# Pooling mixer on plain 32-bit operands, and the last feed-forward's first weights split on VectorE between the norms

## The chip, the cores and the metric

One core of a Trainium2 chip runs the whole program. The metric is the device time of one execution in microseconds (us); a kernel's time is the median of its runs.

## What is computed

One inference step of a backbone of two layers: feed-forward, token mixer, feed-forward, with an RMS norm and a modulation before and an RMS norm and a gate after each. The first layer's mixer is a recurrent scan, the second layer's a pooling mixer. The change is in the pooling mixer and in the feed-forward behind it (the fourth and last). Cut to that:

```python
def rms_norm(x, g):
    return x * lax.rsqrt(jnp.mean(x * x, axis=-1, keepdims=True) + RMS_EPS) * g

def premod(x, g_pre, shift, scale):
    return rms_norm(x, g_pre) * (1 + scale) + shift

def pool_mix(h, pool_w, pool_scale, grid):      # windows 2, 4, 8, 16 for four groups of 256 channels
    for gi, win in enumerate(POOL_WINDOWS):
        part = h[..., gi * POOL_GC:(gi + 1) * POOL_GC]
        m = part
        for ax in axes:
            m = centred_box_mean(m, win, ax)
        outs.append(m - part)
    y = jnp.einsum('...gc,gce->...ge', jnp.stack(outs, axis=-2), pool_w)
    return y.reshape(B, T, D) * pool_scale

        out = pool_mix(h, W['pool_w'][j], W['pool_scale'][j], grid)
        x = x + m[5] * rms_norm(out, W['norm_post'][i, 1])
        h = premod(x, W['norm_pre'][i, 2], m[6], m[7])
        f = (silu(h @ w1) * (h @ w3)) @ w2
        x = x + 0.5 * m[8] * rms_norm(f, W['norm_post'][i, 2])
```

There are 640 tokens (512 on a grid of width 64, and 128 in a row), 1024 channels, and a feed-forward width of 2816.

## The kernel before

Activations lie channels by tokens: `x` is 8 tiles of 128 channels by 640 tokens. The tokens are handled in two halves, half 0 of 384 and half 1 of 256 (`HALF`), nearly everywhere one after the other. Most matmuls are made three times, on operands split into a high and a low part of the type fp32r: high by high, high by low, low by high (`mm3`, lines L299 to L301). So each weight tile of 128x1024 is loaded by a transfer (L290, queue of SyncE), cast to its high part on ScalarE (L293) and has that subtracted on VectorE or GpSimd (L294) (`wsplit`). The table `EARLY` says which of a feed-forward's first weight tiles have the subtraction on GpSimd.

A feed-forward has 22 pieces of 128 rows. Its first part (`ffn_s1`) multiplies the activations by the pieces of w1 and w3, its second (`ffn_s2`) the product by those of w2, half 0 and then half 1. Behind the second part a postnorm (L232 to L243) scales the result and adds it to `x`.

A prenorm squares `x` on ScalarE (L211), adds the squares on VectorE (L215), sums them over channels on TensorE (L178), makes the reciprocal root on VectorE (L181 to L192), spreads it over partitions on TensorE (L194), multiplies `x` by it on VectorE (L257) and applies scale and shift on ScalarE (L266) with a few pieces on GpSimd (L264). `prenorm` then casts each of the 8 tiles to its high part on ScalarE (L275) and subtracts it on VectorE (L276).

The pooling mixer (`PoolMix`) works in another order than the formula, since mixing channels and averaging over tokens commute:

- `load_weights` loads the two tiles of mixing weights, casts them on ScalarE (L1161) and subtracts on VectorE (L1162).
- `mix` multiplies, for each of the five blocks of 128 tokens, the normed activations by them: 8 products of 256 columns for each block, three times each (L1201 to L1203). The result z is cast (L1205) and subtracted (L1206) into a high and a low tile. These ten tiles live in the six pairs of buffers of the feed-forward's split weights ("wh", "wl").
- `window` multiplies z by matrices of zeros and ones that stand for the box sums (L1223). These are loaded (L1169) and converted to fp32r on GpSimd, the last seven on ScalarE (L1171).
- its `postnorm` multiplies by the reciprocal counts (L1234, VectorE), squares (L1237, ScalarE), adds up the squares (L1241, VectorE), and, with the reciprocal root, scales (L1245, VectorE) and adds to `x` (L1247, in turn on GpSimd and VectorE).

The tile framework keeps the engines' queues: a list scheduler sets the order of each engine's instructions when the program is built, each engine then executes its own list strictly in that order, and an instruction waits for the tiles that it reads and for the buffer that it writes. So an instruction that waits holds up all behind it on its engine, and on SyncE's queue a transfer that waits for its buffer holds up those behind it. The raw weight tiles have four buffers.

## Time and profile before

| what | value |
|---|---|
| time, median of 3 runs | 3035.88 us (3034.88 to 3042.86) |
| the profiled execution's own time | 3045.13 us |
| its span, first to last instruction | 3043.2 us |
| TensorE matmul busy | 2860.9 us (94%) |
| VectorE busy | 1836.1 us (60%) |
| ScalarE busy | 1078.8 us (35%) |
| GpSimd busy | 478.8 us (16%) |
| DMA, mean over the span | 126 GB/s |

The profile is one execution. Its engines are PE (TensorE; PEld is its weight load), DVE (VectorE), ACT (ScalarE), POOL (GpSimd) and SP (SyncE). L followed by a number is a line of the kernel before. PEclk is the clock that TensorE was granted, as a share of 2.4 GHz: 1.00 is the upper of its two levels, 0.50 the lower, 1.2 GHz. All times of a timeline count from the start of the span. The pooling stage and the start of the last feed-forward lie between about 2440 and 2600 us.

### The profile page before, as it was taken

To read this page: it belongs to the slowest core of one execution; us is meant where nothing else is said; L and a number is where in the kernel's file an instruction comes from. 1 tells how busy PE (TensorE), PEld (TensorE's weight loads), DVE (VectorE), ACT (ScalarE), POOL (GpSimd) and SP (SyncE) were. 2 spreads that over 40 slices of the span, in tenths; PEclk is the share of its full clock that TensorE was granted. 3 is DMA by queue.
4 is the path that set the end of the run, shared out by engine and by line. 5 is a ranking of instruction groups with operands and counts; after the bars stand their busy time and mean duration, and the time that the engine had idled before them with its cause. 6 is when DMAs were issued, how large, how long until landed. Compare 5 with 4: busy or idle time off the path is not lost.

```text
span 3043.2 us, 52485 instructions
## 1 busy us (share of the span) xinstructions
PE 2860.9 (94%) x21086; PEld 2567.0 (84%) x21086; DVE 1836.1 (60%) x3662; ACT 1078.8 (35%) x1892; POOL 478.8 (16%) x530
## 2 busy tenths in 40 slices
PE   8999999898899999998799999999999986999997
PEld 5999998585566666667689999999999986999997
DVE  7997328835666776664879992763232678423336
ACT  3112234234444454544431123542122454312233
POOL 2000033121001011101400003310002433000034
PEclk9999999998788898887899999999999987999999
DMA  6665234435333443114336663332223432222233
GB/s 245 198 219 179 84 126 142 157 118 167 115 90 107 118 119 113 42 31 139 114 122 212 228 221 132 125 113 81 72 77 111 139 107 80 90 77 70 92 123 125
DMA packets 163733, 382.02 MB, mean 126 GB/s; under 512 B 22433, under 2 KB 84513, under 8 KB 163233
## 3 DMA queue, kind: packets, MB, share of 16 engines
q1 hardware_dynamic: 161472, 375.60, 37.9%
q8 instruction: 165, 2.70, 0.4%
q10 hardware_dynamic: 2016, 3.07, 0.3%
q14 instruction: 80, 0.65, 0.1%
HBM read 352.19 MB, written 26.41 MB: 124 GB/s over the span
## 4 chain that ended last, share of the span: by engine, by line
PE 75%; DVE 12%; ACT 5%; issue 4%; DMA 4%; POOL 1%; SPq 0%; DVEq 0%; ACTq 0%; POOLq 0%
PE ps L300 17%; PE ps L299 17%; PE ps L301 17%; PE px L667 4%; PE pg L811 2%; DVE cj L113 2%; PE pa L739 1%; DVE t L215 1%; PE pc L949 1%; PE px L638 1%; ACT gg L897 1%; DMA mid<-xs 1%; PE ps L502 1%; ACT t L266 1%; DVE wl L294 1%
## 5 line engine op out<-in xcount | busy, mean ns | idle before, releaser
L299 PE MATMUL ps<-hp,wh 128*128 128x384 f32 (+2 forms) x3008 | 934.1, 312 | 17.3 <-ACT hp L275 10.4
L300 PE MATMUL ps<-hp,wh 128*128 128x384 f32 (+2 forms) x3008 | 935.4, 312 | 5.7 <-DVE hp L483 2.1
L301 PE MATMUL ps<-hp,wl 128*128 128x384 f32 (+2 forms) x3008 | 930.9, 310 | 3.3 <-DVE wl L294 3.1
L294 DVE TENSOR_TENSOR wl<-raw,wh 128x1024 fp32r<-128x1024 f32 x353 | 438.7, 1247 | 468.5 <-ACT wh L293 468.0
L293 ACT ACTIVATE wh<-raw 128x1024 fp32r<-128x1024 f32 x369 | 389.4, 1059 | 831.7 <-PE ps L300 693.0
L299 PEld LDWEIGHTS ps<-hp,wh 128*128 128x128 f32 x3008 | 571.0, 190 | 20.9 <-ACT hp L275 12.6
L300 PEld LDWEIGHTS ps<-hp,wh 128*128 128x128 f32 x3008 | 572.7, 190 | 8.2 <-DVE hp L483 2.3
L301 PEld LDWEIGHTS ps<-hp,wl 128*128 128x128 f32 x3008 | 570.0, 190 | 5.6 <-DVE wl L294 5.3
L350 POOL TENSOR_TENSOR gl<-t,gh 128x384 fp32r<-128x384 f32 (+1 forms) x176 | 236.3, 1344 | 1564.4 <-ACT gh L349 1534.3
L301 PE MATMUL ps<-gh,wl 128*128 128x384 f32 (+1 forms) x1408 | 438.3, 312 | 4.1 <-DVE wl L294 4.1
L300 PE MATMUL ps<-gl,wh 128*128 128x384 f32 (+1 forms) x1408 | 436.3, 310 | 3.1 <-POOL gl L350 3.1
L299 PE MATMUL ps<-gh,wh 128*128 128x384 f32 (+1 forms) x1408 | 436.0, 310 | 2.6 <-ACT gh L349 2.6
L113 DVE CUSTOM_DVE_ANT_0 cj<-raw,cj,bmod 128x1024 bf16<-128x1024 f32 x264 | 341.4, 1293 | 13.5 <-DMA raw<-in_w_mod 9.5
L301 PEld LDWEIGHTS ps<-gh,wl 128*128 128x128 f32 x1408 | 269.0, 191 | 5.2 <-DVE wl L294 4.3
L300 PEld LDWEIGHTS ps<-gl,wh 128*128 128x128 f32 x1408 | 268.5, 191 | 5.0 <-POOL gl L350 4.3
L299 PEld LDWEIGHTS ps<-gh,wh 128*128 128x128 f32 x1408 | 268.8, 191 | 4.4 <-ACT gh L349 3.2
L323 ACT ACTIVATE t<-ps 128x384 f32<-128x384 f32 (+1 forms) x176 | 75.5, 429 | 382.2 <-PE ps L301 382.2
L667 PE MATMUL px<-mid,pw 128*128 128x320 f32 x448 | 184.3, 525 | 9.8 <-DMA mid<-xs 7.0
L325 DVE TENSOR_TENSOR t<-t,ps 128x384 f32<-128x384 f32 (+1 forms) x176 | 85.4, 485 | 156.3 <-PE ps L301 155.8
L324 DVE SCALAR_TENSOR_TENSOR t<-t,ps 128x384 f32<-128x384 f32 (+1 forms) x176 | 85.1, 483 | 119.3 <-ACT t L323 119.3
L667 PEld LDWEIGHTS px<-mid,pw 128*128 128x128 f32 x448 | 84.2, 217 | 46.4 <-issue 16.2
L349 ACT ACTIVATE gh<-t 128x384 fp32r<-128x384 f32 (+1 forms) x176 | 79.9, 457 | 53.6 <-PE ps L301 30.2
(372 smaller groups left out, 3444.6 us busy)
## 6 DMA issues: line engine op xcount, KB each, us to landing
raw<-in_w SPq DMA_DIRECT2D x352, 512.0 KB, 3.3
raw<-in_w_mod SPq DMA_DIRECT2D x132, 512.0 KB, 4.2
mid<-xs SPq DMA_DIRECT2D x224, 160.0 KB, 2.3
pw<-in_w_rkv SPq DMA_DIRECT2D x28, 256.0 KB, 3.3
raw<-in_w_o SPq DMA_DIRECT2D x9, 512.0 KB, 5.7
d<-po SPq DMA_DIRECT2D x28, 160.0 KB, 2.3
w<-in_w_mod_first SPq DMA_DIRECT2D x8, 512.0 KB, 7.7
raw<-in_w_rkv SPq DMA_DIRECT2D x8, 512.0 KB, 4.9
```

The costliest lines, as they stand in the source:

```text
L113: nc.vector.tensor_tensor_reduce(self.junk, w, self.cond[:, i], 0.5, self.bmod[:, layer, idx, k:k + 1], ALU.mult, ALU.add, out[:, k, i:i + 1])
L293: nc.scalar.activation(h, w, AF.Copy)
L294: (eng or nc.vector).tensor_tensor(l, w, h, op=ALU.subtract)
L299: nc.tensor.matmul(out, wh, xh, start=start, stop=False)
L300: nc.tensor.matmul(out, wh, xl, start=False, stop=False)
L301: nc.tensor.matmul(out, wl, xh, start=False, stop=stop)
L323: nc.scalar.activation(gt, o[0], AF.Tanh, scale=0.5)
L324: nc.vector.scalar_tensor_tensor(gt, gt, 1.0, o[0], op0=ALU.add, op1=ALU.mult)
L325: nc.vector.tensor_tensor(gt, gt, o[1], op=ALU.mult)
L349: nc.scalar.activation(gh, g, AF.Copy)
L350: nc.gpsimd.tensor_tensor(gl, g, gh, op=ALU.subtract)
L667: nc.tensor.matmul(p[:, 0:320], w[k // 4][:, k % 4 * P:k % 4 * P + P], x, start=k == 0, stop=k == KD - 1)
```

## The change

The mixing weights are loaded as they are and used in 32 bits, and so are the normed activations of the pooling mixer (`prenorm_plain`), so that each product is made once. The casts and subtractions of both go. The mixed tiles z of the fifth block move to the buffer "cj", which is free by then, so that two of the six pairs of weight buffers are free during the mixing. Of the last feed-forward the first three pieces (six weight tiles) are split on VectorE, `EARLY[2]` being empty, and asked for with `fetch` by hand: piece 0 behind half 0's prenorm, piece 1 before half 1's postnorm, piece 2 behind it. Line numbers shift by a few (L294 becomes L300, L1171 L1176, L1234 L1238, L1241 L1245, L1245 L1249, L1247 L1251), and the mixing matmuls are L1207.

```diff
--- before.py
+++ after.py
@@ -35,7 +35,7 @@
 PB = (5, 6, 7, 3, 1, 2, 0, 4)
 SQ = (0, 2, 4, 6)
 XD = (1, 3, 5, 7)
-EARLY = ((), (0, 1, 2, 3, 4, 5), (0, 1, 2, 3, 4, 5))
+EARLY = ((), (0, 1, 2, 3, 4, 5), ())
 
 
 class Net:
@@ -278,6 +278,12 @@
             lo.append(l)
         return hi, lo
 
+    def prenorm_plain(self, hf, gs, sh, bank=None):
+
+        h = [self.part(hf, k, 0, F32) for k in range(KD)]
+        self.prenorm_to(hf, gs, sh, lambda k, _: [(a, b, cd, h[k][:, a:b]) for a, b, cd in SEGS[hf]], bank)
+        return h
+
     def prenorm_to(self, hf, gs, sh, dest, bank=None):
         for _ in self.prenorm_gen(hf, gs, sh, dest, bank):
             pass
@@ -306,9 +312,12 @@
         g = [[None] * NFF, [None] * NFF]
         ws = {}
 
-        def step(f, hf):
+        def fetch(f):
             if f not in ws:
                 ws[f] = [self.wsplit(t["w13"][fi, f, i], nc.gpsimd if 2 * f + i in early else None) for i in range(2)]
+
+        def step(f, hf):
+            fetch(f)
             hi, lo = hs[hf]
             n = HALF[hf][1] - HALF[hf][0]
             o = []
@@ -330,7 +339,7 @@
         order = [(f, h) for h in (lead, 1 - lead) for f in range(3)]
         for f in range(3, NFF):
             order += [(f, 0), (f, 1)]
-        return order, step, g
+        return order, step, g, fetch
 
     def ffn_s2(self, wsrc, gsrc, nk, hf):
         nc, t = self.nc, self.t
@@ -1154,13 +1163,9 @@
         n, nc = self.n, self.nc
         self.ws = []
         for j in range(2):
-            w = n.wp.tile([P, 1024], F32, tag="wh", name=n.name("pw"), bufs=n.nw)
+            w = n.raw([P, 1024])
             nc.sync.dma_start(w, self.t["pool_w"][j])
-            h = n.wp.tile([P, 1024], F32R, tag="raw", name=n.name("pwh"), bufs=n.nraw)
-            l = n.wp.tile([P, 1024], F32R, tag="raw", name=n.name("pwl"), bufs=n.nraw)
-            nc.scalar.activation(h, w, AF.Copy)
-            nc.vector.tensor_tensor(l, w, h, op=ALU.subtract)
-            self.ws.append((h, l))
+            self.ws.append(w)
 
     def load_box(self, hf, lo=0, hi=None):
         n, nc, t = self.n, self.nc, self.t
@@ -1185,22 +1190,21 @@
     def mix(self, hf, h):
 
         n, nc = self.n, self.nc
-        hi, lo = h
         for j in range((HALF[hf][1] - HALF[hf][0]) // P):
-            zh = n.wp.tile([P, 1024], F32R, tag="wh", name=n.name("zh"), bufs=n.nw)
-            zl = n.wp.tile([P, 1024], F32R, tag="wl", name=n.name("zl"), bufs=n.nw)
+            if 3 * hf + j < 4:
+                zh, zl = (n.wp.tile([P, 1024], F32R, tag=s, name=n.name("z"), bufs=n.nw) for s in ("wh", "wl"))
+            else:
+                z = n.main.tile([P, 4 * NT], F32R, tag="cj", name=n.name("z"))
+                zh, zl = z[:, 0:1024], z[:, 1024:2048]
             ts = slice(j * P, (j + 1) * P)
             for q in range(2):
                 p = n.psum()
-                wh, wl = self.ws[q]
                 for g in range(2):
                     for kk in range(2):
                         s = slice((g * 2 + kk) * 256, (g * 2 + kk) * 256 + 256)
                         k = (2 * q + g) * 2 + kk
                         o = p[:, g * 256:g * 256 + 256]
-                        nc.tensor.matmul(o, hi[k][:, ts], wh[:, s], start=kk == 0, stop=False)
-                        nc.tensor.matmul(o, hi[k][:, ts], wl[:, s], start=False, stop=False)
-                        nc.tensor.matmul(o, lo[k][:, ts], wh[:, s], start=False, stop=kk == 1)
+                        nc.tensor.matmul(o, h[k][:, ts], self.ws[q][:, s], start=kk == 0, stop=kk == 1)
                 es = slice(q * 512, q * 512 + 512)
                 nc.scalar.activation(zh[:, es], p, AF.Copy)
                 nc.vector.tensor_tensor(zl[:, es], p, zh[:, es], op=ALU.subtract)
@@ -1266,7 +1270,7 @@
         n.fp, n.ntmp = c.enter_context(tc.tile_pool(name=n.name("fp"), bufs=1)), NFF
 
     def run_ffn(i, hs, todo, l, s, after, wait=0, early=(), begun=None):
-        order, step, g = begun or n.ffn_s1(i, hs, 0, early)
+        order, step, g, _ = begun or n.ffn_s1(i, hs, 0, early)
         todo = list(todo)
         for q, (f, hf) in enumerate(order):
             if g[hf][f] is None:
@@ -1402,7 +1406,7 @@
                 hold["gs"] = gs_sh(1, 1)
             if hf == 1:
                 pm.load_weights()
-            h = n.prenorm(hf, *hold["gs"], bank)
+            h = n.prenorm_plain(hf, *hold["gs"], bank)
             if hf == 0:
                 pm.load_box(0)
                 pm.load_rc(0)
@@ -1417,12 +1421,19 @@
         pm.load_rc(1)
         for hf in range(2):
             pm.mix(hf, hp[hf])
-        hs = []
+        hs = [None, None]
+        begun = n.ffn_s1(3, hs, 0, EARLY[2])
         for hf in range(2):
             o, bank = pm.window(hf)
+            if hf:
+                begun[3](1)
             pm.postnorm(o, hf, gp, bank)
-            hs.append(n.prenorm(hf, gs, sh, bank))
-        run_ffn(3, hs, [], 1, 2, lambda hf, bank: n.store_x(y_out, hf), early=EARLY[2])
+            if hf:
+                begun[3](2)
+            hs[hf] = n.prenorm(hf, gs, sh, bank)
+            if hf == 0:
+                begun[3](0)
+        run_ffn(3, hs, [], 1, 2, lambda hf, bank: n.store_x(y_out, hf), begun=begun)
 
 
 def pack_pool(i):
```

The order of the instructions that results, at two places. First VectorE while half 0's squares are added up behind the pooling mixer (`t_24240`, in the changed kernel `t_24103`, is the sum). Before:

```order
L215 TENSOR_TENSOR t_24240<-t_24240,t_24242 128x384
L1247 TENSOR_TENSOR x_13843<-x_13843,t_24195 128x384
L215 TENSOR_TENSOR t_24240<-t_24240,t_24245 128x384
L1234 TENSOR_TENSOR t_24407<-ps_24343,t_23925 128x256
L215 TENSOR_TENSOR t_24240<-t_24240,t_24248 128x384
L215 TENSOR_TENSOR t_24240<-t_24240,t_24251 128x384
L1234 TENSOR_TENSOR t_24411<-ps_24343,t_23925 128x256
L215 TENSOR_TENSOR t_24240<-t_24240,t_24254 128x384
L215 TENSOR_TENSOR t_24240<-t_24240,t_24257 128x384
L1234 TENSOR_TENSOR t_24416<-ps_24344,t_23927 128x256
L215 TENSOR_TENSOR t_24240<-t_24240,t_24260 128x384
L1241 TENSOR_TENSOR t_24409<-t_24409,t_24413 128x256
```

Now:

```order
L215 TENSOR_TENSOR t_24103<-t_24103,t_24105 128x384
L1251 TENSOR_TENSOR x_13843<-x_13843,t_24058 128x384
L215 TENSOR_TENSOR t_24103<-t_24103,t_24108 128x384
L300 TENSOR_TENSOR wl_24285<-raw_24282,wh_24284 128x1024
L215 TENSOR_TENSOR t_24103<-t_24103,t_24111 128x384
L300 TENSOR_TENSOR wl_24291<-raw_24288,wh_24290 128x1024
L215 TENSOR_TENSOR t_24103<-t_24103,t_24114 128x384
L1238 TENSOR_TENSOR t_24294<-ps_24218,t_23869 128x256
L215 TENSOR_TENSOR t_24103<-t_24103,t_24117 128x384
L1238 TENSOR_TENSOR t_24298<-ps_24218,t_23869 128x256
L215 TENSOR_TENSOR t_24103<-t_24103,t_24120 128x384
L1238 TENSOR_TENSOR t_24303<-ps_24219,t_23871 128x256
```

The two subtractions of piece 1 (`wl_24285`, `wl_24291`) now stand among the additions of the sum; before, the subtractions of these weights were in GpSimd's list.

Second SyncE's queue of transfers while half 1 is mixed and half 0's window runs (`in_w` with the name `raw` is the feed-forward's weights, `in_box_b` the window matrices of half 1). Before:

```order
L1169 DMA t_23897<-in_box_b 128x256
L290 DMA raw_24601<-in_w 128x1024
L290 DMA raw_24607<-in_w 128x1024
L1169 DMA t_23901<-in_box_b 128x256
L290 DMA raw_24667<-in_w 128x1024
L290 DMA raw_24673<-in_w 128x1024
L1169 DMA t_23905<-in_box_b 128x256
L290 DMA raw_24733<-in_w 128x1024
L1169 DMA t_23909<-in_box_b 128x256
L1169 DMA t_23913<-in_box_b 128x256
L1169 DMA t_23917<-in_box_b 128x256
L1169 DMA t_23921<-in_box_b 128x256
```

Now:

```order
L1174 DMA t_23841<-in_box_b 128x256
L1174 DMA t_23845<-in_box_b 128x256
L296 DMA raw_24282<-in_w 128x1024
L296 DMA raw_24288<-in_w 128x1024
L1174 DMA t_23849<-in_box_b 128x256
L296 DMA raw_24379<-in_w 128x1024
L296 DMA raw_24385<-in_w 128x1024
L1174 DMA t_23853<-in_box_b 128x256
L1174 DMA t_23857<-in_box_b 128x256
L1174 DMA t_23861<-in_box_b 128x256
L1174 DMA t_23865<-in_box_b 128x256
```

The two weight tiles of piece 0 no longer stand here; they are asked for earlier, among the first window matrices of half 0. Four weight tiles (pieces 1 and 2) stand where four stood before (pieces 0 and 1), ahead of the last four window matrices.

## Rows read from the trace of the kernel before

**Rows 1.** The page, part 4: the chain that ended last, share by engine.

```profile
PE 75%; DVE 12%; ACT 5%; issue 4%; DMA 4%; POOL 1%; SPq 0%; DVEq 0%; ACTq 0%; POOLq 0%
```

**Rows 2.** Stretches: us, then busy (instructions) of PE, PEld, DVE, ACT, POOL; PEclk, DMA, GB/s.

```profile
2476.80:2487.35 10.55, 9.72 (x81) 9.28 (x80) 9.28 (x32) 4.18 (x9) 0.12 (x1) 1.00 0.05 17
...
2502.90:2510.50 7.60, 7.59 (x48) 7.60 (x49) 4.93 (x14) 7.22 (x20) 1.39 (x2) 0.73 0.21 68
...
2525.95:2545.47 19.52, 3.13 (x15) 2.64 (x13) 19.31 (x23) 10.29 (x17) 15.41 (x9) 0.54 0.33 107
```

**Rows 3.** Timeline of PE at the last feed-forward's start: start, length, line, [idle before <- releaser].

```profile
2545.47 1.44 PE L178 MATMUL ps<-inv_d,t 128*128 128x2 f32 x6 [13.48 <-DVE t L215]
...
2593.15 0.38 PE L300 MATMUL ps<-hp,wh 128*128 128x256 f32 x1 [0.25 <-DVE hp L276]
```

**Rows 4.** Timeline of DVE, half 0's sum of squares behind the pooling mixer.

```profile
2531.56 2.45 DVE L215 TENSOR_TENSOR t<-t,t 128x384 f32<-128x384 f32 x1
...
2535.20 2.70 DVE L215 TENSOR_TENSOR t<-t,t 128x384 f32<-128x384 f32 x1
...
2538.16 4.99 DVE L215 TENSOR_TENSOR t<-t,t 128x384 f32<-128x384 f32 x2
...
2544.86 0.55 DVE L215 TENSOR_TENSOR t<-t,t 128x384 f32<-128x384 f32 x1
2545.33 2.57 DVE L1241 TENSOR_TENSOR t<-t,t 128x256 f32<-128x256 f32 x1
```

**Rows 5.** Timeline of POOL in the same stretch.

```profile
2534.83 7.91 POOL L294 TENSOR_TENSOR wl<-raw,wh 128x1024 fp32r<-128x1024 f32 x3
```

**Rows 6.** Line L294 in the pooling stage, ns min/median/max.

```profile
L294 DVE TENSOR_TENSOR wl<-raw,wh x11: 1216/1226/1824, 2434.9 to 2597.6; 128x1024 fp32r<-128x1024 f32 x11
...
L294 POOL TENSOR_TENSOR wl<-raw,wh x6: 2356/2611/2666, 2512.7 to 2545.0; 128x1024 fp32r<-128x1024 f32 x6
```

**Rows 7.** Timeline of ACT in the pooling stage.

```profile
2446.21 0.92 ACT L275 ACTIVATE hp<-t 128x384 fp32r<-128x384 f32 x2
...
2504.14 1.25 ACT L266 ACTIVATE t<-t,mall,gall 128x128 f32<-128x128 f32 x3
2505.30 0.71 ACT L275 ACTIVATE hp<-t 128x256 fp32r<-128x256 f32 x2
...
2511.55 1.06 ACT L293 ACTIVATE wh<-raw 128x1024 fp32r<-128x1024 f32 x1
```

**Rows 8.** Timeline of PE, third feed-forward's tail.

```profile
2453.57 0.62 PE L299 MATMUL ps<-gh,wh 128*128 128x256 f32 x3 [1.32 <-ACT gh L349]
2454.51 0.39 PE L300 MATMUL ps<-gl,wh 128*128 128x256 f32 x1 [0.32 <-POOL gl L350]
```

**Rows 9.** Timeline of DVE ahead of the third feed-forward's last postnorm.

```profile
2471.08 1.23 DVE L1162 TENSOR_TENSOR pwl<-pw,pwh 128x1024 fp32r<-128x1024 f32 x1 [2.66 <-ACT pwh L1161]
```

**Rows 10.** Timeline of PE in the channel mixing of half 0.

```profile
2482.03 0.28 PE L1201 MATMUL ps<-pwh,hp 128*128 128x256 f32 x1
...
2485.43 0.28 PE L1201 MATMUL ps<-pwh,hp 128*128 128x256 f32 x1
```

**Rows 11.** Timeline of PE: plain 32-bit matmuls at the lower and the upper clock.

```profile
581.71 2.28 PE L502 MATMUL ps<-t,w 128*128 128x382 f32 x3 [8.02 <-DVE t L466]
...
593.79 1.26 PE L502 MATMUL ps<-t,w 128*128 128x260 f32 x5
```

**Rows 12.** Line L502 by stretch: us, busy of PE, of PEld, granted clock, DMA, GB/s.

```profile
582.00:583.00 1.00, 1.00 (x2) 0.55 (x2) 0.50 0.00 0
594.00:595.00 1.00, 1.00 (x5) 0.58 (x4) 1.00 0.50 146
```

**Rows 13.** Line L502, ns min/median/max.

```profile
L502 PE MATMUL ps<-t,w x144: 382/383/1004, 550.7 to 607.6; 128*128 128x260 f32 x80, 128*128 128x382 f32 x64
```

**Rows 14.** The chain of waits in order of time, around half 0's window.

```profile
2511.43 7.48 DMA t<-in_box_b
...
2521.16 0.84 PE ps L178 x6
```

## Prediction

> **What bounds the kernel now.** I read the page's chain of waits first: TensorE holds 75% of it, VectorE 12% [rows 1], so a change outside TensorE pays only where TensorE waits. The change touches one place, about 2440 to 2600 us, so I cut that into stretches [rows 2]. The reader is to see two kinds. While half 0 is mixed (2476.8 to 2487.4) TensorE is busy 9.72 of 10.55 us, but so is VectorE with 9.28. Behind the pooling mixer (2525.95 to 2545.47) TensorE works 3.13 of 19.52 us and VectorE 19.31: there VectorE is the bound. Then the timelines say what the waits end on: TensorE stands still for 13.48 us until the sum of squares L215 is there [rows 3], and this is the longest wait of the place.
>
> **Why VectorE is slow there.** An L215 of 384 columns takes 0.55 us at 2544.86, but 2.45, 2.70 and twice 2.5 us between 2531 and 2543 [rows 4]. In just this time GpSimd subtracts weights, three in 7.91 us [rows 5], and each stretched addition ends about when one of those does. GpSimd's subtraction takes 2.61 us, VectorE's 1.23 [rows 6].
>
> **The change part by part.** My sum is made against the profiled execution's 3045.13 us, which is 9.25 us above the median of 3035.88; I take the same saving off either.
>
> *a. The tail of the third feed-forward.* ScalarE's 8 casts L275 of half 0's activations, 0.46 us each [rows 7], 3.7 us in all, are gone. Behind them in ScalarE's list stood the cast gh for which TensorE waited 1.32 us, and GpSimd's gl after it, 0.32 us [rows 8]. With 3.7 us less ahead of gh both waits vanish: 1.6 us. Bounds: 0 if the next weight is late instead, 1.6 otherwise, since no other wait stands there. VectorE's 8 subtractions go too; they cost nothing here, as TensorE covers them.
>
> *b. The postnorm before the mixing.* VectorE can take the first bank of results only when it is through with L1162, which waits 2.66 us for the cast of the mixing weights and ends at 2472.3 [rows 9]. TensorE finishes one bank of 18 matmuls each 18 x 0.113 = 2.04 us (the spacing of such products: 30 steps from 2482.03 to 2485.43 [rows 10]), the last at 2476.8, so the first was there at 2476.8 - 3 x 2.04 = 2470.7. Without L1162 VectorE starts 1.6 us sooner, and TensorE's list, which has the norm's small matmuls among the mixing, waits on VectorE. I take those 1.6; bounds 0 (another wait takes its place) and 2.
>
> *The mixing matmuls themselves.* Half 0 had 72 products at 0.113 us, 8.1 us; now 24. For a plain 32-bit product the nearest rows are those of the recurrent mixer's projections: five of 260 columns in 1.26 us, three of 382 in 2.28 [rows 11], the former at granted clock 1.00 and the latter at 0.50 [rows 12]. The last of a group runs to its own end, 0.38 us at the shortest and 1.00 at the longest [rows 13], so the spacings are (1.26 - 0.38)/4 = 0.22 us and (2.28 - 1.00)/2 = 0.64, and for 256 columns 0.22 and 0.43. So 24 x 0.22 = 5.3 us, 2.8 us less TensorE work. I count this at nothing, as VectorE's 9.28 us cover it: TensorE only waits longer for the norm in its midst.
>
> *c. Half 1: prenorm, mixing, half 0's window.* TensorE takes each tile as ScalarE casts it, and in the 7.60 us of this mixing ScalarE is busy 7.22 [rows 2]. Eight casts of 0.35 go, 2.8 us; the 12 pieces L266 that stay are 12 x 0.42 = 5.0 us [rows 7]. TensorE now has 16 products for 48: at the lower level 16 x 0.43 = 6.9 us, at the upper 3.5; the stretch had 0.73. Behind it ScalarE has two casts of piece 0 instead of one, 1.06 us more [rows 7], and VectorE two subtractions, 2.4 us, where it had stood waiting for ScalarE. What ended this stretch was a window matrix that landed 7.48 us after it was asked for [rows 14], behind four weight tiles in the queue; the queue has four ahead of it again, the first of them released by the end of the mixing, so it comes earlier as the mixing does. I take 2.8 - 1.1 = 1.7. Bounds: 0 (the matrices land no earlier) and 2.8.
>
> *d. Half 0's sum of squares.* Without GpSimd's subtractions four additions shrink to 0.55 us: (2.45 - 0.55) + (2.70 - 0.55) + (4.99 - 1.10) = 7.9 us. Two subtractions of piece 1 enter VectorE's list among them, 2 x 1.23 = 2.5 us; nothing else there changes its count. 7.9 - 2.5 = 5.4, and I take 5.5 with a little for VectorE's update of `x`. Bounds 3 (ScalarE, which now casts three weight tiles ahead of the last square instead of two, becomes the slower) and 8 (the two fit into gaps).
>
> *e. From that sum to the last feed-forward.* The stretched L1241 ends at 2545.33 + 2.57 = 2547.90 [rows 4], 1.0 us behind TensorE's sums L178, which end at 2545.47 + 1.44 = 2546.91 [rows 3], and the norm's first step waits for it. This 1.0 goes, one subtraction of 1.23 us comes in, and the sixth lies under TensorE's spreading of the norm: -0.2. Bounds -1.2 and 1.0.
>
> *The rest.* Half 1's norm is made while TensorE works on half 0's first pieces; it waited 0.25 us for it [rows 3]. That cover moves along with the start and stays. The end of the kernel is the same.
>
> Sum: 1.6 + 1.6 + 1.7 + 5.5 - 0.2 = **10.2 us**. Profiled 3034.9, median **3025.7**. The bounds add up to 1.8 and 15.4.
>
> **The rivals.** *The transfers hold it.* If the last window matrices come no earlier, or ScalarE's casts of piece 0 and 1 hold the squares, c gives 0 and d 3: 1.6 + 1.6 + 3 - 0.2 = 6.0, 3029.9. For it speaks that the DMA link is the chain's longest single one there, 7.48 us [rows 14], and that ScalarE gets three casts ahead of the last square; against it, that two of the six tiles now land before the mixing.
>
> *Four passes.* Spacing at 0.43 us at the upper level and 0.87 at the lower, if a plain 32-bit product took twice what I read. Mixing half 0 would be 24 x 0.43 = 10.3 us, 2 us more than before, and half 1 about 4 us longer than I reckon: 10.2 - 2 - 4 = 4.2, 3031.7. Against it: 0.22 us for 260 columns at 2.4 GHz are two cycles for a column [rows 11], though this is another place of the kernel. The Trainium skill states this rule (FP8 and Floating Point Precision, section TensorE Precision Notes): true FP32 goes through the array in four passes. The rows here speak against it; by it the time would be that of this rival.
>
> *A ring of waits makes it slower.* ScalarE's cast of piece 1 (wh) stands ahead of five of the eight squares, and its buffer is one that holds z until TensorE's last window matmuls are through; these wait for window matrices that ScalarE converts itself, and whose transfers stand in the queue behind weight tiles that wait for VectorE's subtractions of piece 0. Each us by which the last matrix comes later than I reckon makes the sum of squares a us later: from 10.2 us on the change loses, and at 20 us the time is 3025.7 + 20 = 3045.7. Against it: the worst landing that the chain shows here was 7.48 us [rows 14], with four weight tiles ahead as now.
>
> *More than reckoned.* If the matrices land at once and the two subtractions fit into gaps: 1.6 + 2 + 2.8 + 8 + 1.0 = 15.4, 3020.5.
>
> **How the numbers follow.** About 0.3% (9.1 us) is what a measurement of this kernel can tell from no change, so the bounds of "same" are 3026.8 and 3045.0. My forecast (9.1 to 13 us saved) has 0.45, more than that 0.13: faster 0.58. Transfers or ScalarE 0.27, four passes 0.05, other losses of a and b 0.05: same 0.37. The ring, 0.05: slower. The three runs of before lie 8 us apart, so the range is 3018.5 to 3033.0: it takes in the larger gain and the transfers, and reaches into the four passes, and leaves out some 2 in 10.
>
> **What would show it.** In the changed profile: no wait on gh in the third feed-forward's tail; L1207 spaced 0.22 us at clock 1.00; every L215 of half 0 near 0.55 us, and no GpSimd subtraction of weights between 2500 and 2560; TensorE's wait of 13.48 us down to 7 to 9; about 5 us gained by the first norm behind the window, 10 by the last feed-forward's first matmul. I am wrong if L215 stays above 2 us without GpSimd beside it, if L1207 is spaced 0.43 at clock 1.00, or if the gain of the place is given back within the last feed-forward.

## Result and the profile after

| | before | after |
|---|---|---|
| median of the runs shown together, us | 3034.99 (3028.22 to 3047.93, 12 runs) | 3019.62 (3010.37 to 3034.76, 12 runs) |
| ratio to before, 95% interval | | 0.995 [0.9936, 0.9965] |
| the same kernel timed a second time (run again, below) | 3030.86 (35 runs) | 3021.72 (12 runs), 0.9971 [0.9958, 0.9984] |
| profiled execution, us (its span) | 3045.13 (3043.2) | 3018.19 (3016.4) |
| TensorE busy, us | 2860.9 | 2849.8 |
| VectorE busy, us | 1836.1 | 1821.1 |
| GpSimd busy, us | 478.8 | 462.2 |

The change is faster in both comparisons, by the medians 15.4 us in the first (10.6 to 19.4 by its interval) and 9.1 us in the second (4.9 to 12.7). I had forecast 10.2 us and 3025.7, with a range of 3018.5 to 3033.0.

The page's chain of waits [rows 1]: TensorE's share is up from 75% to 78%, VectorE's down from 12% to 11%.

```profile
PE 78%; DVE 11%; ACT 4%; issue 3%; DMA 3%; POOL 1%; SPq 0%; ACTq 0%; DVEq 0%; POOLq 0%
```

The two profiled executions lie 26.8 us apart in span, but not all of it is the change: 17.8 us stand already at the sums L178 of the norm ahead of the third feed-forward's tail (2435.03 and 2417.22), and up to there both programs issue the same instructions. So I measure from there. Call **the place** the way from these sums to the last feed-forward's first product, and cut it at rows that both traces have: the first mixing product of half 0, that of half 1, the sum of squares behind half 0's window (L178 in six steps), half 0's next sum (L178), the first product.

| stretch, us | before | after | forecast and measured |
|---|---|---|---|
| a: tail of the third feed-forward | 41.88 | 39.50 | 1.6, got 2.4 |
| b and the norm of c: mixing half 0 to mixing half 1 | 26.00 | 24.35 | |
| rest of c: to the sum behind half 0's window | 18.25 | 18.46 | b + c 3.3, got 1.4 |
| d: to half 0's sum of squares | 24.31 | 17.83 | 5.5, got 6.5 |
| e: to the last feed-forward's first product | 11.50 | 11.65 | -0.2, got -0.15 |
| the place | 121.94 | 111.79 | 10.2, got 10.15 |
| from there to the end | 486.23 | 487.39 | 0, got -1.2 |

Three stretches of after in the view of stretches (us; busy and instructions of PE, PEld, DVE, ACT, POOL; granted clock, DMA share, GB/s), for the three of [rows 2]:

```profile
2456.88:2465.91 9.03, 9.01 (x43) 7.53 (x43) 7.47 (x28) 3.54 (x7) 0.00 (x0) 1.00 0.00 1
...
2481.07:2489.78 8.71, 8.71 (x33) 7.44 (x34) 3.75 (x10) 7.15 (x17) 1.34 (x3) 0.82 0.08 31
...
2504.32:2517.36 13.04, 2.19 (x14) 1.70 (x12) 13.04 (x25) 9.12 (x16) 4.76 (x4) 0.65 0.23 75
```

While half 0 is mixed TensorE now works 9.01 of 9.03 us, and in half 1's mixing 8.71 of 8.71. Whether it also sets the pace there, the run one_pass asks below. Behind half 0's window TensorE still stands while VectorE is busy from end to end, but for 13.04 us in place of 19.52.

TensorE's timeline at the waits of [rows 3, 8], with what ended each in brackets:

```profile
2449.45 0.38 PE L306 MATMUL ps<-gl,wh 128*128 128x256 f32 x1 [0.64 <-POOL gl L359]
...
2517.36 1.44 PE L178 MATMUL ps<-inv_d,t 128*128 128x2 f32 x6 [8.43 <-DVE t L215]
2524.90 1.65 PE L194 MATMUL ps<-dg,ones 128*128 128x384 f32 x2 [6.10 <-DVE dg L192]
...
2529.01 1.33 PE L305 MATMUL ps<-hp,wh 128*128 128x384 f32 x3 [1.82 <-ACT hp L275]
```

The wait of 1.32 us on gh and that of 0.32 us on gl behind it are gone. The 0.64 us on gl are those of the tail's last piece, which the kernel before has too (0.43 us at 2469.44; the prediction left it out). The 13.48 us for the sum of squares are 8.43. The same timeline in the mixing, for [rows 10], and under it all of line L1207 (ns, shortest, median, longest):

```profile
2456.72 4.05 PE L1207 MATMUL ps<-raw,hp 128*128 128x256 f32 x18
...
2481.07 8.71 PE L1207 MATMUL ps<-raw,hp 128*128 128x256 f32 x32 [1.07 <-POOL hp L264]
```

```profile
L1207 PE MATMUL ps<-raw,hp x80: 377/379/796, 2456.7 to 2489.4; 128*128 128x256 f32 x80
```

The source has 40 products at L1207, the trace 80 matmul records: a plain 32-bit product leaves two. 18 records in 4.05 us, the last of 0.38, are (4.05 - 0.38) / 17 = 0.216 us for a record and 0.43 for a product, at a granted clock of 1.00. My 0.22 us for a product was the time of a record.

VectorE's timeline through half 0's sum of squares and the first steps of the norm behind it, for [rows 4]:

```profile
2509.92 0.84 DVE L215 TENSOR_TENSOR t<-t,t 128x384 f32<-128x384 f32 x1
...
2511.15 0.55 DVE L215 TENSOR_TENSOR t<-t,t 128x384 f32<-128x384 f32 x1
2511.62 1.21 DVE L300 TENSOR_TENSOR wl<-raw,wh 128x1024 fp32r<-128x1024 f32 x1
2512.75 0.55 DVE L215 TENSOR_TENSOR t<-t,t 128x384 f32<-128x384 f32 x1
2513.22 1.22 DVE L300 TENSOR_TENSOR wl<-raw,wh 128x1024 fp32r<-128x1024 f32 x1
...
2515.16 0.55 DVE L215 TENSOR_TENSOR t<-t,t 128x384 f32<-128x384 f32 x1
...
2519.66 0.16 DVE L183 TENSOR_SCALAR ms<-ms 128x3 f32<-128x3 f32 x1
2519.73 0.15 DVE L186 TENSOR_TENSOR a<-yi 128x3 f32<-128x3 f32 x1
2519.80 0.42 DVE L1238 TENSOR_TENSOR t<-ps,t 128x256 f32<-128x256 f32 x1
2520.14 0.15 DVE L187 TENSOR_TENSOR a<-a,ms 128x3 f32<-128x3 f32 x1
2520.20 1.22 DVE L300 TENSOR_TENSOR wl<-raw,wh 128x1024 fp32r<-128x1024 f32 x1
```

No L215 takes more than 0.84 us. The one of 0.84 us ends at 2510.76, 0.41 us after an addition of GpSimd:

```profile
2509.10 1.25 POOL L1251 TENSOR_TENSOR x<-x,t 128x384 f32<-128x384 f32 x1 [0.26 <-DVE t L1249]
```

Among VectorE's additions stand the two subtractions that I had counted, and the norm's small steps (L183 to L187) take turns with half 1's L1238 and another subtraction. The chain of waits around half 0's window (start, length), for [rows 14]:

```profile
2481.07 8.71 PE ps L1207 x32
2489.78 9.73 PE ps L1227 x65
2499.53 0.84 PE ps L178 x6
```

TensorE's own products follow each other here; the window matrix, whose landing was a link of 7.48 us before, isn't in the chain any more.

### The profile page after: what moved, and what is told of

It reads as the page before. It is cut to its first block, busy times and chain, and to the rows that moved or that the text cites. A ratio compares the mean times of both kernels' runs of the same rounds, so it can differ in the third digit from the quotient of the medians.

```text
span 3016.4 us, 52355 instructions
## 1 busy us (share of the span) xinstructions
PE 2849.8 (94%) x21046; PEld 2557.6 (85%) x21046; DVE 1821.1 (60%) x3650; ACT 1070.1 (35%) x1874; POOL 462.2 (15%) x524
## 4 chain that ended last, share of the span: by engine, by line
PE 78%; DVE 11%; ACT 4%; issue 3%; DMA 3%; POOL 1%; SPq 0%; ACTq 0%; DVEq 0%; POOLq 0%
PE ps L306 18%; PE ps L305 18%; PE ps L307 18%; PE px L676 4%; PE pg L820 2%; DVE cj L113 2%; PE pa L748 1%; PE pc L958 1%; PE px L647 1%; DVE t L215 1%; ACT gg L906 1%; DMA mid<-xs 1%; PE ps L511 1%; DVE wl L300 1%; PE pc L966 1%
## 5 line engine op out<-in xcount | busy, mean ns | idle before, releaser
L305 PE MATMUL ps<-hp,wh 128*128 128x384 f32 (+2 forms) x3008 | 932.2, 312 | 15.0 <-ACT hp L275 10.4
L300 DVE TENSOR_TENSOR wl<-raw,wh 128x1024 fp32r<-128x1024 f32 x359 | 446.8, 1248 | 472.6 <-ACT wh L299 471.9
L305 PEld LDWEIGHTS ps<-hp,wh 128*128 128x128 f32 x3008 | 569.5, 190 | 18.4 <-ACT hp L275 12.2
L113 DVE CUSTOM_DVE_ANT_0 cj<-raw,cj,bmod 128x1024 bf16<-128x1024 f32 x264 | 341.4, 1293 | 12.8 <-DMA raw<-in_w_mod 8.8
```

The costliest lines, as they stand in the source:

```text
L113: nc.vector.tensor_tensor_reduce(self.junk, w, self.cond[:, i], 0.5, self.bmod[:, layer, idx, k:k + 1], ALU.mult, ALU.add, out[:, k, i:i + 1])
L300: (eng or nc.vector).tensor_tensor(l, w, h, op=ALU.subtract)
L305: nc.tensor.matmul(out, wh, xh, start=start, stop=False)
```

## Experiments

All places and ends below come from one profile each. The sum of both is the best figure, as it leaves out what lies ahead. The two executions of the changed kernel (after and again) differ by 0.1 us in the place and by 1.6 us in the sum, so sums that lie 2 us apart tell little.

| run | a | b, norm | rest of c | d | e | place | to the end | sum |
|---|---|---|---|---|---|---|---|---|
| before | 41.88 | 26.00 | 18.25 | 24.31 | 11.50 | 121.94 | 486.23 | 608.2 |
| after | 39.50 | 24.35 | 18.46 | 17.83 | 11.65 | 111.79 | 487.39 | 599.2 |
| again | 39.73 | 24.34 | 18.38 | 17.79 | 11.66 | 111.90 | 485.70 | 597.6 |
| gpsimd_splits | 38.70 | 25.33 | 19.66 | 24.17 | 10.77 | 118.63 | 486.75 | 605.4 |
| vector_splits | 41.75 | 25.02 | 18.00 | 17.02 | 13.25 | 115.04 | 486.75 | 601.8 |
| plain_only | 39.61 | 25.43 | 19.38 | 24.19 | 10.77 | 119.38 | 486.49 | 605.9 |
| no_early_fetch | 39.65 | 24.27 | 19.82 | 17.03 | 12.76 | 113.53 | 484.65 | 598.2 |
| one_pass | 39.73 | 24.45 | 17.68 | 18.30 | 11.66 | 111.82 | 487.94 | 599.8 |
| norm_first | 39.90 | 23.81 | 19.92 | 15.54 | 8.99 | 108.16 | 498.17 | 606.3 |

**again: the changed kernel once more.** No edit.

> The changed kernel, unchanged. Call the place the stretch of TensorE's work from its first product behind the last sum of squares of half 0's norm ahead of the third feed-forward's tail to the last feed-forward's first product: 120.3 us in the profile of before, 109.9 in that of after. The two profiles lie 26.9 us apart, though, and 17.6 of this stand already ahead of the place, where the two programs are the same. Theory A: what lies ahead differs from execution to execution, and the change is worth what the place and the last feed-forward show, 9 to 10.5 us; the median then comes to 0.9965 to 0.997 of before, and in the traces of these four kernels the start of the place scatters by 10 us or more without regard to the edit. Theory B: the whole difference of the medians, 15.4 us, belongs to the change (something ahead of the place runs faster); then the ratio comes to 0.995 again, and the place starts about 5 us or more sooner in every kernel with plain operands. Within the place both expect 109.9 +- 1.

Measured: 3021.72 us, ratio 0.9971 [0.9958, 0.9984]. The place is 111.9 us (1.9 less in the count of the expectation, which begins at the first product behind the sums). In the nine profiles of the table it starts at 2435.0, 2417.2, 2421.3, 2429.4, 2419.7, 2416.3, 2423.4, 2413.9 and 2411.1 us, in the table's order, though no edit touches what lies ahead. Theory B wanted an earlier start with plain operands, but gpsimd_splits, with them, starts at 2429.4 and vector_splits, without them, at 2419.7. So theory A holds: 9.0 and 10.6 us by the sums are the change, and the profiles differ by up to 24 us ahead of it, those of the changed kernel alone by 4.1.

**gpsimd_splits: the subtractions back on GpSimd.**

```diff
-EARLY = ((), (0, 1, 2, 3, 4, 5), ())
+EARLY = ((), (0, 1, 2, 3, 4, 5), (0, 1, 2, 3, 4, 5))
```

> The changed kernel with the weights of the last feed-forward's first three pieces subtracted on GpSimd again. Theory 1 (an addition of VectorE is stretched while GpSimd subtracts): three or more of half 0's L215 take 2.4 us or more again, the place takes 115 to 118 us (6.5 us of the 10.4 are lost), the time rises by 5 to 8 us against the changed kernel. Theory 2 (the additions waited for something else, such as ScalarE's squares, and the earlier fetch cured it): L215 stays at 0.55 to 0.85 us, the place at 110 +- 1.

VectorE's timeline of this run in half 0's sum of squares, then GpSimd's:

```profile
2523.50 2.33 DVE L215 TENSOR_TENSOR t<-t,t 128x384 f32<-128x384 f32 x1
...
2527.03 2.71 DVE L215 TENSOR_TENSOR t<-t,t 128x384 f32<-128x384 f32 x1
...
2529.99 4.98 DVE L215 TENSOR_TENSOR t<-t,t 128x384 f32<-128x384 f32 x2
```

```profile
2523.07 2.35 POOL L300 TENSOR_TENSOR wl<-raw,wh 128x1024 fp32r<-128x1024 f32 x1 [0.66 <-ACT wh L299]
...
2526.65 7.91 POOL L300 TENSOR_TENSOR wl<-raw,wh 128x1024 fp32r<-128x1024 f32 x3
```

Four L215 are at 2.3 to 2.7 us again, each through about 0.4 us after one of GpSimd's subtractions (the second: 2527.03 + 2.71 = 2529.74, against 2526.65 + 7.91 / 3 = 2529.29). Stretch d is 24.17 us, as before. Theory 1 holds for the additions and the place. The time is another matter: the median is 11.3 us above that of again, where 5 to 8 were expected and the sums say 6.2 and 7.8. The ratio, 1.001 [0.9999, 1.0021], says 3 us slower than before where the sum says 2.8 us faster; that much may lie ahead of the place, and why isn't settled.

**vector_splits: the kernel before, with VectorE's splits alone.**

```diff
-EARLY = ((), (0, 1, 2, 3, 4, 5), (0, 1, 2, 3, 4, 5))
+EARLY = ((), (0, 1, 2, 3, 4, 5), ())
```

> The kernel before with nothing changed but the engine of the last feed-forward's six first subtractions: VectorE for GpSimd. Theory 1: half 0's L215 near 0.55 us, the place falls from 120.3 to 113 to 115.5 us, 5 to 7 us. Theory 2: the place stays within 1.5 us of 120.3, since the raw weights come as late as before and VectorE now has them to subtract as well.

TensorE's timeline in the third feed-forward's tail and at half 0's sum:

```profile
2437.85 0.61 PE L299 MATMUL ps<-gh,wh 128*128 128x256 f32 x3 [1.04 <-ACT gh L349]
...
2521.50 1.44 PE L178 MATMUL ps<-inv_d,t 128*128 128x2 f32 x6 [6.70 <-DVE t L215]
```

The sum's wait is halved, the wait on gh is there as before. Stretch d gains 7.3 us, e loses 1.75, since three subtractions stand in the norm's chain: the place gains 6.9 us, sum 6.4. Ratio 0.9991 [0.9976, 1.0006]. Theory 1 holds.

**plain_only: the kernel before, with the plain mixing alone.**

```diff
...
-            h = n.prenorm(hf, *hold["gs"], bank)
+            h = n.prenorm_plain(hf, *hold["gs"], bank)
...
-                        nc.tensor.matmul(o, hi[k][:, ts], wh[:, s], start=kk == 0, stop=False)
-                        nc.tensor.matmul(o, hi[k][:, ts], wl[:, s], start=False, stop=False)
-                        nc.tensor.matmul(o, lo[k][:, ts], wh[:, s], start=False, stop=kk == 1)
+                        nc.tensor.matmul(o, h[k][:, ts], self.ws[q][:, s], start=kk == 0, stop=kk == 1)
```

> The kernel before with the plain 32-bit channel mixing alone; the splits stay on GpSimd and the last feed-forward's weights are asked for where they were. Theory 1: the place takes 116 to 117 us (2.6 us off the third feed-forward's tail, 0.7 off the postnorm, 0.8 off half 1's way, and the stretched additions stay). Rival (the plain products, of which the profile of after shows two matmul records each, 0.43 us for a product, cost what the casts saved): within 1 us of 120.3.

TensorE's wait at half 0's sum in this run:

```profile
2524.94 1.44 PE L178 MATMUL ps<-inv_d,t 128*128 128x2 f32 x6 [13.79 <-DVE t L215]
```

It is as long as before. Stretch a gains 2.3 us, the mixing 0.6 and e 0.7, the rest of c loses 1.1, for a reason that no run here shows: the place gains 2.6. In the count of the expectation it is 117.5 us, between the two: theory 1 said 116 to 117, the rival 119.3 or more. The tail's 2.6 us came as theory 1 said, the other 1.5 did not. Ratio 0.9999 [0.9983, 1.0015], too wide for a sum of 2.3 us.

**no_early_fetch: the change without its calls between the norms.**

```diff
-        begun = n.ffn_s1(3, hs, 0, EARLY[2])
...
-            if hf:
-                begun[3](1)
...
-            if hf:
-                begun[3](2)
...
-            if hf == 0:
-                begun[3](0)
-        run_ffn(3, hs, [], 1, 2, lambda hf, bank: n.store_x(y_out, hf), begun=begun)
+        run_ffn(3, hs, [], 1, 2, lambda hf, bank: n.store_x(y_out, hf), early=EARLY[2])
```

> The changed kernel without its calls that ask for the last feed-forward's pieces between the norms: plain mixing and VectorE's splits stay, the pieces are asked for where the kernel before did. The place, now counted from the sums L178 of half 0's norm ahead of the third feed-forward's tail to the last feed-forward's first product, is 121.9 us before, 111.8 and 111.9 in two profiles of the change. Theory 1 (the two other parts make the gain: VectorE's splits alone gave 6.9, plain mixing alone 2.6, together 9.5 of the 10.1): 111.5 to 113. Rival (the calls matter, as the weights would otherwise be asked for too late): 114 to 116, and TensorE waits for a weight in the last feed-forward's first pieces.

```profile
2524.19 1.44 PE L178 MATMUL ps<-inv_d,t 128*128 128x2 f32 x6 [6.71 <-DVE t L215]
...
2536.95 1.97 PE L305 MATMUL ps<-hp,wh 128*128 128x384 f32 x5 [3.31 <-ACT hp L275]
```

These are TensorE's waits at half 0's sum and at the first product: 1.7 us less at the one, 1.5 more at the other than in after, as one of VectorE's subtractions has moved from the sum to the norm behind it. The rest of c is 1.4 us longer. The place is 1.7 us longer than in after, between the ranges of the two theories, the way to the end 2.7 shorter, the sum 598.2, between the two of the change. Ratio 0.9971 [0.9956, 0.9985]. The calls move work about and gain nothing that these runs can tell.

**one_pass: what the plain product's price is worth.** The channel mixing is done on operands rounded to the type of the other products; the low halves are left out.

```diff
-        h = [self.part(hf, k, 0, F32) for k in range(KD)]
+        h = [self.part(hf, k, 0) for k in range(KD)]
...
-            w = n.raw([P, 1024])
-            nc.sync.dma_start(w, self.t["pool_w"][j])
+            w = n.wp.tile([P, 1024], F32R, tag="raw", name=n.name("raw"), bufs=n.nraw)
+            nc.gpsimd.dma_start(w, self.t["pool_w"][j])
```

> The changed kernel with the channel mixing's operands rounded to the type of the other products, once each: half 0's activations by ScalarE's write, the weights by a transfer that GpSimd asks for. It leaves out the low halves, so the output is less exact. It prices the plain product: one matmul record of 0.113 us at clock 1.00 for each product in place of two of 0.214. Theory 1 (the mixing's TensorE time lies beside VectorE's and ScalarE's, whose 7.5 and 7.2 us of it stay): mixing half 0 to the sum behind the window gains 1 to 3 us, no more, the place 109 to 111. Rival (the price of the plain product is on the path in full): 24 x 0.32 + 16 x 0.32 = 12.8 us or more gained, the place at 99 or less.

Line L1207 of this run, and TensorE's waits behind the mixing:

```profile
L1207 PE MATMUL ps<-raw,hp x40: 276/276/582, 2453.7 to 2482.3; 128*128 128x256 f32 x40
```

```profile
2469.02 1.59 PE L1227 MATMUL ps<-t,z 128*128 128x256 f32 x4 [5.60 <-DVE t L1238]
...
2514.10 1.44 PE L178 MATMUL ps<-inv_d,t 128*128 128x2 f32 x6 [11.79 <-DVE t L215]
```

Forty records now, for forty products, and half 0's 24 take 2.88 us in place of 48 x 0.216 = 10.4. Yet the place is 111.82 us: TensorE waits 5.60 us for VectorE's L1238, and 11.79 us for half 0's sum in place of 8.43. Only the rest of c gains, 0.8 us, and d gives half of it back. In half 0 VectorE's list covers the price in full: to half 1's mixing it is 24.45 us, against 24.35.

In half 1 it does not. The 16 products take 4.78 us where after had 8.71, as long as ScalarE's L266, which makes their operands (4.72 us), at a granted clock of 0.50. VectorE's last L1245 ahead of the sum, in after and then here:

```profile
2498.92 0.56 DVE L1245 TENSOR_TENSOR t<-t,t 128x384 f32<-128x384 f32 x1 [0.28 <-ACT t L1241]
```

```profile
2493.65 0.56 DVE L1245 TENSOR_TENSOR t<-t,t 128x384 f32<-128x384 f32 x1 [0.22 <-ACT t L1241]
```

It ends 18.4 us behind half 1's first product in after and 16.1 us behind it here, 2.3 us sooner. But the order built for this run has 78 window products ahead of the sum where after had 65, and TensorE reaches it 1.6 us after that L1245. So as built the price of the plain product is worth 0.8 us in the rest of c and 0.7 from half 0's mixing on, below theory 1's 1 to 3 and far from the rival's 12.8. In an order without the 13 extra products it would be some 2.3 us, an estimate from these two rows. The place, 111.82, is outside both ranges.

**norm_first: half 0's norm ahead of half 1's work.**

```diff
-                begun[3](1)
-            pm.postnorm(o, hf, gp, bank)
+                with tc.issue_after(n.last):
+                    begun[3](1)
+                    pm.postnorm(o, hf, gp, bank)
+            else:
+                pm.postnorm(o, hf, gp, bank)
```

(`n.last` is the last L192 of half 0's norm; `issue_after` puts VectorE's instructions of the block behind it.)

> The changed kernel with VectorE's work on half 1's postnorm and on piece 1's weights queued behind the last step of half 0's norm ahead of the last feed-forward. Theory 1 (VectorE's list is the bound of both stretches: two subtractions of 1.22 us and three pieces of half 1 among the sum of squares, eleven among the norm's chain, which took 5.3 us where the same chain took 2.2 us by itself): the sum comes 3 us sooner, the norm 3 us more, the place takes 105 to 107. What becomes of it: theory 1a (half 1's norm is covered) the end gains the 5 to 6 us too; theory 1b (VectorE's work up to half 1's norm is the same, so it is ready no sooner) TensorE waits 4 to 6 us for half 1's operands behind half 0's three pieces and the end gains 0 to 1.5. Rival (the chain is slow for another reason): place 111 +- 1.

TensorE's waits at half 0's sum, at its norm, and then within the last feed-forward; and one stretch of it:

```profile
2510.24 1.44 PE L178 MATMUL ps<-inv_d,t 128*128 128x2 f32 x6 [5.22 <-DVE t L215]
2514.69 1.65 PE L194 MATMUL ps<-dg,ones 128*128 128x384 f32 x2 [3.00 <-DVE dg L192]
...
2551.57 0.61 PE L178 MATMUL ps<-inv_d,t 128*128 128x2 f32 x4 [3.17 <-DVE t L215]
2554.97 1.22 PE L194 MATMUL ps<-dg,ones 128*128 128x256 f32 x2 [2.80 <-DVE dg L192]
2558.05 1.44 PE L305 MATMUL ps<-hp,wh 128*128 128x256 f32 x5 [1.85 <-ACT hp L275]
```

```profile
2545.00:2570.00 25.00, 17.18 (x110) 16.05 (x109) 15.79 (x47) 11.90 (x29) 4.10 (x6) 0.80 0.00 1
```

The first two fall to 5.22 and 3.00 us, and the first product comes 3.6 us sooner, less than the 5 to 7 expected. But behind half 0's three pieces TensorE waits 3.17 + 2.80 + 1.85 = 7.8 us for half 1's norm, and the granted clock is 0.80 from 2545 to 2570, where after had 1.00 from 2555 to 2580. Counted from the start of the place, the end lies 7.1 us behind that of after: theory 1b, and worse. Ratio 0.9983 [0.9968, 0.9998].

**second_too and second_all: the same move in the second feed-forward.** There GpSimd subtracts weights beside VectorE too. In the profile of after, VectorE's timeline, then GpSimd's:

```profile
1451.42 2.46 DVE L239 TENSOR_TENSOR t<-t,t 128x256 f32<-128x256 f32 x1
...
1454.33 5.13 DVE L239 TENSOR_TENSOR t<-t,t 128x384 f32<-128x384 f32 x3
...
1478.02 2.00 DVE L182 TENSOR_SCALAR yi<-ms 128x2 int32<-128x2 int32 x1
...
1483.40 2.32 DVE L186 TENSOR_TENSOR a<-y 128x2 f32<-128x2 f32 x1
```

```profile
1451.20 7.51 POOL L300 TENSOR_TENSOR wl<-raw,wh 128x1024 fp32r<-128x1024 f32 x3 [3.52 <-ACT wh L299]
...
1477.65 2.35 POOL L300 TENSOR_TENSOR wl<-raw,wh 128x1024 fp32r<-128x1024 f32 x1 [5.75 <-issue]
1483.18 2.53 POOL L300 TENSOR_TENSOR wl<-raw,wh 128x1024 fp32r<-128x1024 f32 x1 [3.18 <-DVE y L188]
```

L182 is a step of 0.16 us on 128 x 2 elements; this one ends at 1480.02, GpSimd's subtraction at 1480.00. The L186 ends at 1485.72, GpSimd's at 1485.71.

```diff
-EARLY = ((), (0, 1, 2, 3, 4, 5), ())
+EARLY = ((), (), ())
```

> The changed kernel with the same move made in the second feed-forward: its first six subtractions on VectorE for GpSimd. In the profile of after, between 1451 and 1488 us, six of GpSimd's subtractions stand beside VectorE's L239 (2.46, and three in 5.13 us, where 0.42 and 0.55 are usual), one L243 of 2.37 us and two steps of a norm's chain of 2.00 and 2.32 us, where 0.16 is usual. Theory 1 (the overlap is what costs, wherever it occurs): VectorE gets back about 11.8 us and takes on 6 x 1.22 = 7.3; TensorE, which waits 5.2, 2.2 and 6.0 us there for VectorE's sums, reaches half 0's first product (1518.03, 97.0 us behind its L1071 of 1421.02) 3 to 5 us sooner, and the end gains 2 to 5. Rival (VectorE's list is full there, busy 66 of 75 us, so what it takes on weighs as much as it gets back): within 1.5 us.

TensorE's waits there, in after and then in second_too:

```profile
1459.05 1.01 PE L178 MATMUL pm<-inv_d,t 128*128 128x2 f32 x4 [5.19 <-DVE t L239]
...
1483.55 1.44 PE L178 MATMUL ps<-inv_d,t 128*128 128x2 f32 x6 [5.99 <-DVE t L239]
...
1518.03 1.97 PE L305 MATMUL ps<-hp,wh 128*128 128x384 f32 x5 [2.46 <-ACT hp L275]
```

```profile
1459.68 0.61 PE L178 MATMUL pm<-inv_d,t 128*128 128x2 f32 x4 [0.19 <-DVE t L239]
...
1479.17 1.01 PE L178 MATMUL pm<-inv_d,t 128*128 128x2 f32 x4 [6.81 <-DVE t L215]
...
1515.61 1.97 PE L305 MATMUL ps<-hp,wh 128*128 128x384 f32 x5 [2.47 <-ACT hp L275]
```

The sums' waits of 5.19, 2.2 and 5.99 us, 13.3 in all, have become 0.19, 6.81 and none, 7.0 in all. From TensorE's L1071 (at the end of the recurrent mixer; L1062 in the kernel before) to half 0's first product (the last row of each) it is 1515.61 - 1425.94 = 89.7 us, against 97.0 in after and 96.8 to 100.0 in the nine profiles of the table above. From L1071 to the start of the place it is 987.0 us against 996.2, so the gain is kept. Median 3012.18, ratio 0.992 [0.9895, 0.9945]: faster than before by 24 us, and than the change by 7 us or more in the profile. Theory 1 holds, with more than the 3 to 5 us expected.

In second_all the output projection's splits go to VectorE as well:

```diff
-WV = ((1, 0), (1, 0), (1, 0), (1, 0))
+WV = ((1, 1), (1, 1), (1, 1), (1, 1))
```

> The same, and the splits of the output projection's weights that GpSimd makes (four 128 x 1024 tiles) on VectorE too, so that GpSimd subtracts no weights at all. Theory 1: each GpSimd subtraction avoided gives VectorE 1.8 to 2 us back and takes 1.22, so 2 to 3 us more than the run beside it. Rival: TensorE waits there for weights (0.77 and 0.58 us for VectorE's splits already in the profile of after), and the projection's get later in VectorE's list: 1 to 4 us lost against the run beside it.

90.2 us to half 0's first product, 987.5 to the place, ratio 0.9912 [0.9889, 0.9936]: no difference from second_too that can be told. Neither theory's 2 us is there.

## Why the forecast held, and which step failed

*a* was right in its cause: without the 8 casts the wait on gh is gone, in all runs with plain operands and in none without. It was too small, 2.4 us for 1.6. TensorE's waits in the stretch fall from 2.07 us to 0.64; the other 0.95 us is TensorE's own work, 39.81 us busy before and 38.86 after, at a mean granted clock of 0.92 and 0.93. I had capped the term at the waits.

*The mixing matmuls* is the step that failed. I read a spacing of records in [rows 11 to 13] as that of products and took 0.22 us; it is 0.43. [rows 13] could have told: they count 80 records of 260 columns where the source makes 40 products (five projections of eight). This was the sign that I named for being wrong, and the rival of four passes was right about the product. The Trainium skill's rule (FP8 and Floating Point Precision, section TensorE Precision Notes: true FP32 takes four passes) agrees with the trace: by it, 256 columns at the upper level, 2.4 GHz, are an estimated 0.427 us, and two records of 0.216 were measured.

I counted the matmuls at nothing, as VectorE covers them. one_pass bears that out for half 0 alone. In half 1 the price went into c: I had reckoned ScalarE's 5.0 us for this mixing, with TensorE's 16 products at 3.5 us at the upper level and 6.9 at the lower. It took 8.71 us, and with the product at a quarter of the price 4.78. The difference of 3.9 is the 4 us that the rival named for half 1. The rival's time, 4.2 us saved, was wrong all the same: its 2 us for half 0 are not there, and of half 1's, by one_pass, only 0.8 (as built) to some 2.3 (estimated) reach the sum behind the window.

*b and c* got 1.4 us for 3.3. Mixing half 0 to half 1 gained 1.65: 0.6 up to half 1's postnorm, 0.4 in half 1's sum (four L178 take 1.01 us at granted clock 0.50 before, 0.61 at 1.00 after), and 0.7 from the norm to the mixing, where the cast is gone. b was too large: VectorE's first L232 starts 5.64 us ahead of the mixing now, waiting for TensorE alone, and started 4.68 ahead of it before, so L1162 had held it up by 1.0 us and not by 1.6. The rest of c lost 0.2: half 1's mixing takes 8.71 us where it took 7.76, by the price above, and the way from there to the sum is 0.7 us shorter. The window matrix is off the chain, which I had not forecast, and TensorE's own products take its place. So neither the rival of the transfers nor the ring of waits came: the matrices that TensorE still waits for, 2.42 us, are half 1's, and it then waits 8.43 us for half 0's sum anyway.

*d* was right, and the largest: 6.5 us for 5.5. vector_splits, which does this part alone, gains 7.3 there; gpsimd_splits, which undoes it alone, loses 6.3. VectorE's addition runs at its 0.55 us when GpSimd doesn't work beside it, and at 2.3 to 2.7 when GpSimd subtracts. Of the 1.0 us more than forecast, 0.8 is VectorE's update of `x` beside a GpSimd addition (L1247, 1.34 us before and 0.55 after), for which I had put in a little. The Trainium skill (SBUF — State Buffer, section Who interferes with whom) says that a VectorE instruction with two SBUF inputs contends with a GpSimd instruction that reads SBUF; the trace agrees, with 0.55 us alone and an end about 0.4 us after GpSimd's when together.

*e* was right, -0.15 for -0.2. The cover of half 1's norm held, but with nothing to spare: TensorE waits 0.78 us for its sum in after (0.69 before, which the prediction left out), and norm_first, which starts 3.6 us sooner, loses all of it there.

So the place came out at 10.15 us for 10.2, partly by luck: a and d gave 1.8 us more, b and c 1.9 less. The first comparison's 15.4 us is nearest to the rival "more than reckoned", but the place shows 10.15 and 10.04 us, and the second comparison 9.1; I take the excess for what executions differ by ahead of the place. That is the likeliest reading, and gpsimd_splits leaves open whether two programs can differ there by a few us for good.

## What to carry to other kernels

An operation moved from GpSimd to VectorE can cost VectorE less than nothing: count what VectorE's neighbours lose while GpSimd works, from the longest and shortest of the same instruction. A term hidden under another engine should be priced twice, once as read and once at double, to see whether the cover holds; here it did in half 0's mixing and not in half 1's. Before a group's time is divided by its records, the records are to be counted against the products in the source: a plain 32-bit product left two. Where two executions of one program differ by more than the change, measure between two rows that both traces have, around the edit, and then on to the end.

## What the runs showed that was not expected

- A plain 32-bit product of 256 columns is two matmul records of 0.216 us at a granted clock of 1.00; a product of the rounded type is one record, at 0.113 [rows 10].
- GpSimd's subtraction stretches not only VectorE's additions: an L182 with one input of 128 x 2 elements took 2.00 us in place of 0.16, and ended with it to 0.02 us.
- Up to the place, nine profiles of programs that issue the same instructions there span 2411.1 to 2435.0 us.
